# First FFN's up-projection by one level of Strassen's scheme, on one NeuronCore

## The chip, the cores and the metric

The kernel runs on one NeuronCore of a Trainium2 chip. The metric is device time in microseconds for one execution of the whole program, as the median of several runs. The engines are TensorE (matmul; PE in the profile, its weight loads PEld), VectorE (DVE), ScalarE (ACT), GpSimd (POOL) and SyncE (SP), which here issues all DMAs. TensorE writes to PSUM, which ScalarE and VectorE read; GpSimd works on SBUF alone.

## The reference

Two layers of a hybrid backbone: 256 context tokens and 512 latent tokens (768 together, `T`), width 1024. Layer 0 is differential attention beside RWKV-7 with a ConvFFN, layer 1 a bidirectional Mamba-2 mixer with a ConvFFN. The change concerns the ConvFFN of layer 0, which runs on all 768 tokens:

```python
FFN_HIDDEN = 2816

def conv_ffn(h, w_up, conv_w, conv_b, w_down):
    val, gate = jnp.split(h @ w_up, 2, axis=-1)
    gate = dwconv_centred(gate, conv_w, conv_b)      # 3 taps along the tokens
    return (jax.nn.silu(gate) * val) @ w_down

# layer 0, for latent and for context tokens
h_lat = modulate(rmsnorm(x_lat, norm_ffn[i]), sh2_l, sc2_l)
x_lat = x_lat + g2_l * conv_ffn(h_lat, ffn_w_up[i], ...)
```

The hidden width 2816 is 22 tiles of 128, so the up-projection has 22 gate tiles and 22 value tiles, each the product of a 1024 x 128 slice of `w_up` with the 1024 x 768 input, and the down-projection has 8 output tiles over 22 input tiles.

## The kernel before

All activations lie transposed: features on the 128 partitions, tokens along the free axis. A product in full precision is made of three matmuls in `fp32r`: weights and activations are each split into a high part (a ScalarE copy to `fp32r`) and a low part (the remainder, by VectorE or GpSimd, function `split`), and the kernel sums high x high, high x low and low x high in PSUM. So an up-projection tile is 8 blocks of 128 input features x 3 matmuls, each over 768 tokens. A matmul's output stays within one PSUM bank of 512 columns, and `DSEG = ((256, 0, NCTX), (512, NCTX, T))` cuts the 768 tokens into a piece of 256 (context) and one of 512 (latent). A dense PSUM tile is 1024 columns, two banks, and the FFN has three of them in turn (`dense_ps`).

`wload` (L192) loads a weight slice of 512 KB by SP into one of two buffers `ws`; `split` writes `wh` (L134, ScalarE) and `wl` (L150, VectorE), two buffers each. `mm3` (L208) does the matmuls of a tile.

`ffn` runs three groups of 8, 8 and 6 hidden tiles. For each hidden tile `j` it makes the gate tile, applies bias and three taps (one ScalarE instruction and four VectorE instructions, read from PSUM, into `fg`), the silu, then makes the value tile, multiplies (L137, VectorE) and splits the product into `ah` and `al`. After a group come its down-projection tiles: 8 tiles of output, each `nk` blocks x 3 matmuls, added to the residual stream by two VectorE instructions (`residual`, L146, one for each token segment with its own modulation). The first three tiles (gate 0, value 0, gate 1) run while the norm before is still being applied: `seg_start` works through a first segment of tokens (L1143, and L1169 for the third tile) while the second segment's `NormMod.steps` modulate it. The last group's down-projection (L1207) goes through `seg_tail`, which interleaves it with the sums of squares (L319), the broadcast of the norm's row (L277) and the modulation of the next norm; its first two output tiles run together (`pair`), over all blocks but the last first.

The program is written in one order; a planner in the tile framework then fixes each engine's own order and the buffers when the program is built, by which instruction is ready first, and among ready ones by the order of the program. On the chip each engine follows that fixed order.

The mixer of layer 1 has the same pieces of 256 and 512 (L1427); its `dt` projection (L1774) alone uses pieces of 384.

## Time and profile before

| | |
|---|---|
| runs | 2375.05, 2375.70, 2380.39 us; median 2375.7 |
| profiled execution, span | 2375.0 us (the lowest of the runs is 0.05 above it) |
| TensorE busy | 2219.4 us, 93% |
| VectorE, ScalarE, GpSimd busy | 58%, 42%, 14% |
| first FFN, by the chain | about 826 to 1390 us |
| its full up-projection and down-projection after the first tiles | 853.0 to 1336.4 us as one unbroken chain of matmuls |
| DMA, mean of the core | 91 GB/s |

The page's slices are fortieths of the span, about 59 us each, so the first FFN is slices 14 to 23. A matmul's busy time overlaps that of the next one, since matmuls are pipelined; the distance from start to start is what it costs in a full stream.

### The profile page before, as it was taken

The page shows a single profiled execution, that of the slowest core. Times are in us where ns is not written, and L with a number is a line of the kernel's source. Part 1 is how long each engine was busy: PE and PEld are TensorE (multiplying, and loading weights), DVE is VectorE, ACT ScalarE, POOL GpSimd, SP SyncE. Part 2 cuts the span into 40 slices and gives each one's busy share as a digit, 9 for nine tenths or more (in the row PEclk, how much of TensorE's full clock was granted, in tenths as well). Part 3 has the DMA queues.
Part 4 walks back from the last instruction along what each step waited for, and adds up shares of the span by engine and source line. Part 5 has one row for each costly group of instructions (what it writes and reads, how often), then busy time and mean ns, then how long its engine had stood idle before and what let it go on. Part 6 is the DMA issues. An engine that isn't in the chain of part 4 may idle for free.

```text
span 2375.0 us, 38460 instructions
## 1 busy us (share of the span) xinstructions
PE 2219.4 (93%) x15644; PEld 1876.9 (79%) x15644; DVE 1382.7 (58%) x2513; ACT 1003.5 (42%) x1904; POOL 341.1 (14%) x358
## 2 busy tenths in 40 slices
PE   6989998688879899999999998999999998999998
PEld 4878887576768788888888886878788877888887
DVE  4777737848585643333323468867676666434445
ACT  4655538474743442122212345544444544323233
POOL 2000006242500110000000022223222123000000
PEclk9999999799979999999999999999899999999999
DMA  8111222767455512222222301111111112333332
GB/s 276 47 43 49 90 98 78 227 205 231 126 174 152 157 55 62 62 62 64 61 64 61 97 23 45 45 45 54 54 54 54 36 45 63 107 96 95 95 97 88
DMA packets 302128, 216.09 MB, mean 91 GB/s; under 512 B 8832, under 2 KB 272640, under 8 KB 301952
## 3 DMA queue, kind: packets, MB, share of 16 engines
q1 hardware_dynamic: 301952, 213.64, 29.8%
q8 instruction: 123, 2.02, 0.4%
q14 instruction: 53, 0.43, 0.1%
HBM read 197.36 MB, written 16.25 MB: 90 GB/s over the span
## 4 chain that ended last, share of the span: by engine, by line
PE 77%; DVE 11%; ACT 5%; DMA 3%; issue 2%; POOL 1%; SPq 1%; DVEq 0%; ACTq 0%; POOLq 0%
PE dps L208 41%; PE dps L1427 9%; PE dps L1207 3%; PE dps L1420 3%; DMA aws<-in_ada_w 2%; PE adaps L957 1%; PE g L724 1%; PE aps L983 1%; PE dps L1143 1%; PE tps L517 1%; DVE cv L146 1%; PE g L673 1%; PE c L851 1%; DVE gl L137 1%; DVE xw L137 1%
## 5 line engine op out<-in xcount | busy, mean ns | idle before, releaser
L134 ACT ACTIVATE wh<-ws 128x1024 fp32r<-128x1024 f32 x196 | 207.9, 1061 | 605.8 <-PE dps L208 469.5
L208 PE MATMUL dps<-hl,wh 128*128 128x256 f32 (+1 forms) x1368 | 402.1, 355 | 0.0
L208 PE MATMUL dps<-hh,wh 128*128 128x256 f32 (+1 forms) x1368 | 399.9, 353 | 1.1 <-ACT vT L134 0.9
L208 PE MATMUL dps<-hh,wl 128*128 128x256 f32 (+1 forms) x1368 | 400.8, 355 | 0.0
L208 PEld LDWEIGHTS dps<-hh,wl 128*128 128x128 f32 x1368 | 257.2, 189 | 37.9 <-issue 0.3
L150 DVE TENSOR_TENSOR wl<-ws,wh 128x1024 fp32r<-128x1024 f32 x136 | 166.7, 1226 | 205.9 <-ACT wh L134 201.9
L208 PEld LDWEIGHTS dps<-hh,wh 128*128 128x128 f32 x1368 | 257.2, 190 | 37.0 <-ACT vT L134 1.3
L208 PEld LDWEIGHTS dps<-hl,wh 128*128 128x128 f32 x1368 | 257.5, 189 | 35.0 <-issue 0.3
L1355 POOL TENSOR_TENSOR wl<-ws,wh 128x1024 fp32r<-128x1024 f32 x52 | 125.2, 2409 | 320.5 <-ACT wh L134 273.2
L1427 PE MATMUL dps<-hh,wh 128*128 128x256 f32 (+1 forms) x448 | 146.9, 380 | 15.4 <-DVE sz L146 13.6
L1427 PE MATMUL dps<-hh,wl 128*128 128x256 f32 (+1 forms) x448 | 142.8, 371 | 0.0
L1427 PE MATMUL dps<-hl,wh 128*128 128x256 f32 (+1 forms) x448 | 142.6, 370 | 0.0
L146 DVE SCALAR_TENSOR_TENSOR cv<-dps,cwh,cv 128x511 f32<-128x511 f32 (+3 forms) x176 | 109.6, 623 | 30.6 <-ACT cv L134 28.1
L208 PE MATMUL dps<-al,wh 128*128 128x512 f32 (+1 forms) x384 | 116.4, 358 | 0.0
L208 PE MATMUL dps<-ah,wl 128*128 128x512 f32 (+1 forms) x384 | 116.1, 357 | 0.0
L208 PE MATMUL dps<-ah,wh 128*128 128x512 f32 (+1 forms) x384 | 114.9, 354 | 0.0
L137 DVE TENSOR_TENSOR fg<-fg,dps 128x768 f32<-128x768 f32 (+1 forms) x44 | 36.1, 821 | 133.0 <-PE dps L208 130.3
L1427 PEld LDWEIGHTS dps<-hh,wh 128*128 128x128 f32 x448 | 86.8, 197 | 32.0 <-DVE sz L146 15.0
L1427 PEld LDWEIGHTS dps<-hh,wl 128*128 128x128 f32 x448 | 87.8, 197 | 13.6
L1427 PEld LDWEIGHTS dps<-hl,wh 128*128 128x128 f32 x448 | 87.9, 197 | 12.9
L146 DVE SCALAR_TENSOR_TENSOR fg<-dps,par,fg 128x511 f32<-128x511 f32 (+1 forms) x132 | 85.1, 658 | 16.4 <-ACT fg L134 14.0
L146 DVE SCALAR_TENSOR_TENSOR x<-dps,mod,x 128x256 f32<-128x256 f32 (+1 forms) x56 | 31.9, 594 | 104.1 <-PE dps L208 102.3
(575 smaller groups left out, 4546.0 us busy)
## 6 DMA issues: line engine op xcount, KB each, us to landing
aws<-in_ada_w SPq DMA_DIRECT2D x96, 512.0 KB, 5.0
ws<-in_ffn_w_up SPq DMA_DIRECT2D x88, 512.0 KB, 3.8
ws<-in_ssm_w_in SPq DMA_DIRECT2D x40, 512.0 KB, 3.9
ws<-in_ffn_w_down SPq DMA_DIRECT2D x32, 512.0 KB, 3.6
ws<-in_ev_w_in SPq DMA_DIRECT2D x26, 512.0 KB, 4.0
ws<-in_ssm_w_out SPq DMA_DIRECT2D x16, 512.0 KB, 3.4
ws<-in_ffn_w_down SPq DMA_DIRECT2D x16, 384.0 KB, 3.1
projd<-tsh SPq DMA_DIRECT2D x12, 384.0 KB, 2.6
```

Of the source, the lines that this page charges most:

```text
L134: S.activation(out=o, in_=i, func=func, bias=bias, scale=scale, **kw)
L137: V.tensor_tensor(out=o, in0=x, in1=y, op=op)
L146: V.scalar_tensor_tensor(out=o, in0=x, scalar=s, in1=y, op0=op0, op1=op1)
L150: eng.tensor_tensor(out=lo, in0=src, in1=hi.bitcast(F32), op=ALU.subtract)
L208: PE.matmul(ps[:, po:po + hi - lo], lhsT=w[:, k0 + k, :], rhs=x[:, xk0 + k, lo:hi], start=(first and k == 0 and j == 0), stop=(last and k ...
L517: PE.matmul(po[:, 0:n], lhsT=w[:, kk, :], rhs=xx[:, kk, 0:n], start=(kk == 0 and j == 0), stop=(kk == nk // 128 - 1 and j == 2))
L673: PE.matmul(zp[:, mm], lhsT=lora[:, d, m * 128:(m + 1) * 128], rhs=wv, start=True, stop=True)
L724: PE.matmul(gp[:, m, :], lhsT=g1[:, m, cl].rearrange("p s t -> p (s t)"), rhs=z[:, m, par_, :], start=True, stop=True)
L1207: PE.matmul(ps[:, off + lo:off + hi], lhsT=w[:, k, :], rhs=x_[:, lo:hi], start=(k == 0 and j == 0), stop=(k == nk - 1 and j == 2))
L1355: G.tensor_tensor(out=lo, in0=w, in1=hi.bitcast(F32), op=SUB)
L1420: PE.matmul(ps[:, 512 * h:512 * h + 512], lhsT=w[:, k, h * 128:(h + 1) * 128], rhs=x[k], start=(k == 0 and j == 0), stop=(k == 3 and j == 2))
L1427: PE.matmul(ps[:, po:po + hi - lo], lhsT=w[:, k, :], rhs=x[:, k, lo:hi], start=(k == 0 and j == 0), stop=(k == KD - 1 and j == 2))
```

## The change

In layer 0's FFN, `ffn` is replaced by `ffn_fast`. Pairs 0 and 1 (value and gate tile of one hidden tile) stay plain. For the other 20 pairs the product of the 256 x 1024 weights (value and gate rows) with the 1024 x 768 input is taken as a 2 x 2 by 2 x 2 block product (blocks: value/gate; first and second half of the input features; first and second 384 tokens) in the Winograd form of Strassen's scheme: seven half products instead of eight, each 4 blocks x 3 matmuls over 384 columns.

- The input's sums and differences are made once (`NormHalf` and `operands`): GpSimd adds high and low parts of the first 384 tokens back together, VectorE makes four differences for each of four feature blocks, and they are split into high and low parts.
- The weights' sums are made for every pair (`fast`): two GpSimd and two VectorE instructions of 512 columns, and a third split, of 1536 columns. The split sums lie in columns 384 to 768 of the first four blocks of `hs`, which no product reads.
- The seven products are combined into value and gate in SBUF: two ScalarE copies, five VectorE sums that read PSUM, two GpSimd sums. The taps then read the gate from SBUF.
- Each product takes half a dense PSUM tile.
- The groups become (0,3), (3,6), (6,10), (10,14), (14,18), (18,22). The down-projection loads weights for two output tiles at a time (`wsplit2`) in the first five groups; the last one runs every output tile by segment, without `pair`.
- Pieces of 256 and 512 become two of 384 in layer 0's input projection, in the FFN and in the mixer (`DSEG`, `XS`), and PSUM offsets move from 256 to 128 for them. The norm ahead of the FFN has segments of 384 (context and the first 128 latent tokens; the other 384).
- The residual stream is held in two tiles, `xc` (context) and `xl` (latent), from the start, loaded by 16 DMAs instead of 8; the weight pool `wsp` is opened once for layer 0's tail and once for layer 1.

```diff
+SEG_MID = (((1, 0, NCTX), (0, NCTX, T // 2)), (0, T // 2, T))
...
-        DSEG = ((256, 0, NCTX), (512, NCTX, T))
+        DSEG = ((128, 0, T // 2), (512, T // 2, T))
...
+        class NormHalf(NormMod):
+            def steps(self, si):
...
+                for q in range(4):
+                    yield
+                    u = self.alloc(F32).rearrange("p (i t) -> p i t", i=2)
+                    for i in range(2):
+                        k = q + 4 * i
+                        stt(u[:, i], self.xv(k, lo, hi), am[:, self.layer, self.which, k, c:c + 1], rs, MUL, MUL)
+                        act(u[:, i], u[:, i], AF.Identity, bias=mod[:, self.layer, 24 * self.which + k, c:c + 1])
+                    split(hh[:, q:q + 5:4, lo:hi], hl[:, q:q + 5:4, lo:hi], u, G)
+                    self.h1.append(u)
+                for q in range(4):
+                    v = self.alloc(F32).rearrange("p (i t) -> p i t", i=2)
+                    G.tensor_tensor(out=v, in0=hh[:, q:q + 5:4, 0:lo].bitcast(F32), in1=hl[:, q:q + 5:4, 0:lo].bitcast(F32), op=ADD)
+                    self.h0.append(v)
+
+            def operands(self):
...
+                    tt(v[:, 0], u[:, 0], v[:, 0], SUB)
+                    tt(u[:, 0], u[:, 1], u[:, 0], SUB)
+                    tt(u[:, 1], u[:, 1], v[:, 0], SUB)
+                    tt(v[:, 1], v[:, 1], u[:, 1], SUB)
...
+                        split(hi, lo, f)
...
+            def prod(w, x):
+                ps = half_ps()
+                for q in range(4):
+                    xh, xl_ = x(q)
+                    for j, (w_, x_) in enumerate(((w[0], xh), (w[0], xl_), (w[1], xh))):
+                        PE.matmul(ps, lhsT=w_[:, q, :], rhs=x_, start=q == 0 and j == 0, stop=q == 3 and j == 2)
+                return ps
...
+            def fast(j):
+                w1 = wload(up[:, j * 128:(j + 1) * 128], KD, 128)
+                w2 = wload(up[:, (NH + j) * 128:(NH + j + 1) * 128], KD, 128)
+                s = pool.tile([128, 4, 3, 128], F32, tag="sw", name="sw", bufs=1)
+                G.tensor_tensor(out=s[:, :, 0], in0=w2[:, 0:4], in1=w2[:, 4:8], op=ADD)
+                tt(s[:, :, 1], s[:, :, 0], w1[:, 0:4], SUB)
+                G.tensor_tensor(out=w2[:, 0:4], in0=w1[:, 0:4], in1=w2[:, 0:4], op=SUB)
+                tt(s[:, :, 2], w1[:, 4:8], s[:, :, 1], SUB)
+                (h1, l1), (h2, l2) = ([wsp.tile([128, 8, 128], F32R, tag=tg, name=tg, bufs=2) for tg in ("wh", "wl")] for _ in range(2))
+                sh, sl = (x[:, 0:4, H:n].rearrange("p k (i m) -> p k i m", i=3) for x in hs)
+                split(h1, l1, w1)
+                split(sh, sl, s)
+                split(h2, l2, w2)
+                g, v, t = fg(), fg(), fg()
+                p5 = pnq.tile([128, 512], F32, tag="nt", name="p5", bufs=3)[:, 0:H]
+                v0, v1, g0, g1 = v[:, 0:H], v[:, H:n], g[:, 0:H], g[:, H:n]
+                act(v0, prod((h1[:, 0:4], l1[:, 0:4]), quad(0, 0)), AF.Copy)
+                act(p5, prod((sh[:, :, 0], sl[:, :, 0]), diff(0, 0)), AF.Copy)
+                tt(v1, v0, prod((sh[:, :, 1], sl[:, :, 1]), diff(1, 1)), ADD)
+                tt(v0, v0, prod((h1[:, 4:8], l1[:, 4:8]), quad(1, 0)), ADD)
+                tt(g1, v1, prod((h2[:, 0:4], l2[:, 0:4]), diff(1, 0)), ADD)
+                G.tensor_tensor(out=v1, in0=v1, in1=p5, op=ADD)
+                tt(v1, v1, prod((sh[:, :, 2], sl[:, :, 2]), quad(1, 1)), ADD)
+                tt(g0, g1, prod((h2[:, 4:8], l2[:, 4:8]), diff(0, 1)), ADD)
+                G.tensor_tensor(out=g1, in0=g1, in1=p5, op=ADD)
+                gate_tail(j, g, t)
+                tt(t, t, v, MUL)
+                return t
+
+            for j0, j1 in ((0, 3), (3, 6), (6, 10), (10, 14), (14, 18), (18, 22)):
...
-                    nm1, fw = ffn(0, x, nm0, fw, SEG_ALL, T, DSEG, pf, next0, prep1, lambda m, si: xsrc(m, *SEG_ALL[si][1:]))
+                    nm1, fw = ffn_fast(0, xv0, nm0, fw, SEG_ALL, T, pf, next0, prep1)
...
-                XS = ((256, 0, NCTX), (512, NCTX, T))
+                XS = ((128, 0, T // 2), (512, T // 2, T))
```

More of the change, by code (lines that the diff above doesn't have):

```diff
@@ L305, in __init__, with add @@
                 self.acc = pool.tile([128, n], F32, tag="nacc" + nm, name="nacc", bufs=1)
-            def add(self, xk):
-                if self.first:
-                    act(self.acc, xk, AF.Square)
-                else:
+            def add(self, *xs):
+                sq = self.acc
+                if not self.first:
                     sq = self.pool.tile([128, max(512, self.n)], F32, tag="nt", name="nsq", bufs=3)[:, 0:self.n]
-                    act(sq, xk, AF.Square)
+                o = 0
+                for xk in xs:
+                    act(sq[:, o:o + xk.shape[-1]], xk, AF.Square)
+                    o += xk.shape[-1]
+                if not self.first:
                     tt(self.acc, self.acc, sq, ADD)
@@ L1076, in add @@
             def add(self, m, si):
-                self.sq[si].add(self.xv(m, *self.segs[si][1:]))
+                self.sq[si].add(*[self.xv(m, lo, hi) for c, lo, hi in self.segs[si]])
             def rows(self, si):
@@ L1081, in rows @@
                     self.banks = (self.psf(), self.psf())
-                c, lo, hi = self.segs[si]
-                sums = self.banks[0 if self.segs[0][2] - self.segs[0][1] < self.segs[1][2] - self.segs[1][1] else 1]
-                return self.sq[si].finish(sums[:, 256 + 64 * si:320 + 64 * si], self.banks[si][:, 0:hi - lo])
+                ns = [hi - lo for lo, hi in self.span]
+                sums = self.banks[0 if ns[0] < ns[1] else 1]
+                return self.sq[si].finish(sums[:, 384 + 64 * si:448 + 64 * si], self.banks[si][:, 0:ns[si]])
@@ L1086, in steps @@
             def steps(self, si):
                 rs = self.rows(si)
-                c, lo, hi = self.segs[si]
+                s0 = self.span[si][0]
                 for k in range(KD):
                     yield
-                    modulate1(self.pool, self.xv(k, lo, hi), self.hs, rs, self.layer, self.which, c, k, lo, hi)
+                    for c, lo, hi in self.segs[si]:
+                        modulate1(self.pool, self.xv(k, lo, hi), self.hs, rs[:, lo - s0:hi - s0], self.layer, self.which, c, k, lo, hi)
@@ L1145, in dense_block, with wsplit2, ffn @@
             return f
+        def wsplit2(src, k, m):
+            w, hi, lo = (wsp.tile([128, 8, 128], t, tag=tg, name=tg, bufs=2).rearrange("p k m -> p (k m)")[:, 0:k * m].rearrange("p (k m) -> p k m", m=m)
+                         for tg, t in (("ws", F32), ("wh", F32R), ("wl", F32R)))
+            SY.dma_start(out=w, in_=src.rearrange("(k p) m -> p k m", p=128))
+            split(hi, lo, w)
+            return hi, lo
         def upw(layer, col, eng=V):
             return wsplit(a["ffn_w_up"][layer][:, col * 128:(col + 1) * 128], KD, eng)
[L1150 removed]
+        def ffn(layer, xv, nm, fw, segs, n, msegs, pool, make_next, prep_next):
             off = 1024 - n
[L1152 removed]
+            moff = msegs[0][0] - msegs[0][1]
+            hs = nm.hs
             dn = a["ffn_w_down"][layer]
```

224 lines of the change are left out of this document (169 added, 55 removed).

## The prediction

> **What bounds the kernel now.** I read the page first (busy shares, slices), then the busy time by stretch, then the chain of waits, then the groups by shape.
>
> ```profile
> PE 2219.4 (93%) x15644; PEld 1876.9 (79%) x15644; DVE 1382.7 (58%) x2513; ACT 1003.5 (42%) x1904; POOL 341.1 (14%) x358
> ...
> PE   6989998688879899999999998999999998999998
> ...
> PEclk9999999799979999999999999999899999999999
> ...
> 853.00:970.00 117.00, 117.00 (x664) 101.41 (x664) 45.89 (x57) 32.99 (x36) 0.00 (x0) 1.00 0.22 64
> ...
> 1346.00:1395.00 49.00, 47.95 (x272) 41.64 (x271) 29.69 (x54) 20.04 (x33) 3.62 (x4) 1.00 0.24 65
> ```
>
> The slices show TensorE full in the middle, where the first FFN lies. The stretch 853 to 970 us (up-projection of the first group; columns: length, busy PE, PEld, DVE, ACT, POOL, granted clock, DMA share, GB/s) has TensorE busy for 117.00 of 117.00 us at full clock, VectorE for 39%, GpSimd for none; in 1346 to 1395 (last down-projection and the start of the next norm) only 1.05 us are idle. So this stage costs its matmuls and nothing else. What one matmul costs is read from the chain, which runs through them back to back:
>
> ```profile
> 815.97 2.44 PE dps L208 x10
> ...
> 818.41 0.44 PE rsps L277 x4
> ...
> 853.00 483.36 PE dps L208 x2736
> ...
> 1412.09 7.30 PE rsps L1774 x42
> ...
> L1774 PE MATMUL rsps<-hh,wd 128*128 128x384 f32 x32 | 7.3, 336 | 0.0
> ```
>
> Third row: 483.36 us / 2736 = 176.7 ns, the mean of a 256 and a 512 column piece. Fourth: 7.30 / 42 = 173.8 ns for a 384 column piece (shape in the fifth row). 768 columns cost 353.3 ns now and 347.6 ns in two pieces of 384.
>
> **The change, TensorE's part.** Before: 44 up tiles of 48 matmuls and 22 x 8 x 3 x 2 = 1056 down matmuls, 3168 x 176.7 = 559.7 us. After: two plain pairs 4 x 48 = 192; twenty pairs of 7 products x 4 x 3 = 84, 1680; down-projection of the first five groups 18 x 48 = 864. These 2736 are 384 wide: 475.5 us. The last group keeps its segments of 512 and 256, 192 matmuls at the mean of both forms, 33.9 us. Together 509.4, so **-50.3 us of TensorE time**; 47.2 of it is the scheme (96 x 176.7 = 16.96 against 84 x 173.8 = 14.60 us a pair).
>
> The Trainium skill ("TensorE: Matmul & The Clock Gate", § Wait — 56ns, not 53.3ns?) puts a warm matmul at N/2.4 GHz plus about 2.5 ns. By it both cuts of 768 columns cost 325 ns, the pieces bring nothing, and the scheme brings 20 x 12 x 162.5 ns = 39 us (an estimate from that page; the total would be 11 us later, 2367). The rows here show 173.8 and 176.7 ns, so the trace disagrees and decides.
>
> **The vector engines' part.** This is what the scheme pays with.
>
> ```profile
> L150 DVE TENSOR_TENSOR wl<-ws,wh 128x1024 fp32r<-128x1024 f32 x136 | 166.7, 1226 | 205.9 <-ACT wh L134 201.9
> ...
> L150 DVE TENSOR_TENSOR wd<-wdt,wd 128x1536 fp32r<-128x1536 f32 x1 | 1.7, 1744 | 0.0
> ...
> L146 DVE SCALAR_TENSOR_TENSOR fg<-dps,par,fg 128x511 f32<-128x511 f32 x88 | 65.8, 747 | 15.6 <-ACT fg L134 14.0
> ...
> L146 DVE SCALAR_TENSOR_TENSOR fg<-dps,par,fg 128x255 f32<-128x255 f32 x44 | 21.1, 479 | 0.8
> ...
> L150 DVE TENSOR_TENSOR al<-fg,ah 128x768 fp32r<-128x768 f32 x22 | 20.9, 952 | 0.9 <-ACT ah L134 0.9
> ...
> L150 DVE TENSOR_TENSOR al<-fg,ah 128x512 fp32r<-128x512 f32 x22 | 15.1, 685 | 1.4 <-ACT ah L134 1.4
> ...
> L137 DVE TENSOR_TENSOR hst<-hst,sps 128x512 f32<-128x512 f32 x12 | 8.2, 681 | 1.4 <-PE sps L1598 0.8
> ...
> L137 DVE TENSOR_TENSOR st<-c,st 128x256 f32<-128x256 f32 x22 | 9.2, 418 | 21.1 <-PE c L851 21.1
> ...
> L134 ACT ACTIVATE wh<-ws 128x1024 fp32r<-128x1024 f32 x196 | 207.9, 1061 | 605.8 <-PE dps L208 469.5 <-issue 63.0 <-PE dps L1427 38.4
> ...
> L134 ACT ACTIVATE wd<-wdt 128x1536 fp32r<-128x1536 f32 x1 | 1.5, 1493 | 0.1
> ...
> L134 ACT ACTIVATE fg<-dps,par 128x768 f32<-128x768 f32 x22 | 21.5, 978 | 2.3 <-PE dps L208 2.3
> ...
> L134 ACT ACTIVATE ah<-fg 128x768 fp32r<-128x768 f32 x22 | 18.6, 848 | 12.3 <-DVE fg L137 12.2
> ...
> L1355 POOL TENSOR_TENSOR wl<-ws,wh 128x1024 fp32r<-128x1024 f32 x52 | 125.2, 2409 | 320.5 <-ACT wh L134 273.2 <-PE dps L1427 12.2 <-DVE er L141 10.4
> ...
> 393.96 1.29 POOL L699 TENSOR_TENSOR br<-kd,slr 128x512 f32<-128x512 f32 x1
> ...
> 394.00 1.80 DVE L137 TENSOR_TENSOR g<-ta,sg 128x512 f32<-128x512 f32 x1 [0.18 <-ACT sg L134]
> ...
> 505.52 3.25 POOL L819 TENSOR_TENSOR st<-st,wc 128x256 f32<-128x256 f32 x1 [4.19 <-DVE vv L137]
> ...
> 505.82 0.68 DVE L146 SCALAR_TENSOR_TENSOR ta<-ta,slkk 128x512 f32<-128x512 f32 x1
> ...
> 507.62 0.68 DVE L137 TENSOR_TENSOR g<-kd,sg 128x512 f32<-128x512 f32 x1
> ```
>
> VectorE per fast pair, both inputs in SBUF: two sums of 512 (2 x 0.685), low halves of w1 and w2 (2 x 1.226) and of the sums (1.744), taps, now from SBUF (2 x 0.69 + 2 x 0.42, by the 512 row and the 256 row; the PSUM rows 747 and 479 ns are the upper end), product and low half (2 x 0.952): 9.7 us. Five evacuations of 384 with one PSUM input, between 0.418 and 0.681, 0.55 each: 2.75. Sum **12.4 us of 14.6**, against 39% now. GpSimd: two of 512 (1.29) and two of 384 (by the 512 and 1024 rows 1.29 and 2.41, 2.2 ns a column: 1.02): **4.6 us**. ScalarE: 2 x 1.061 + 1.493 + 0.978 + 2 x 0.848 and two copies of about 0.49: 7.3 us, not a bound.
>
> The 394.00 row matters: a VectorE operation that takes 0.685 took 1.80, because GpSimd was at 393.96 in a two-input operation of 1.29; at 505.52 it is the other way round, GpSimd stretched to 3.25 while VectorE's operations, back to back, kept 0.68. Two-input work from SBUF on the two engines excludes itself: 9.7 + 4.6 = **14.3 us of exclusive time in a pair of 14.6**. It fits only because a group also has a down-projection (4 x 48 x 173.8 ns = 33.4 us), into which the last pair's tail and the first pair's preparation spread.
>
> **What TensorE then waits for.** Each wait has cover and price; engine changes cost 0.04 to 0.1 us, and the reader of a finished sum starts 0.27 us after TensorE goes on:
>
> ```profile
> 1081.44 0.52 PE L208 MATMUL dps<-hh,wl 128*128 128x256 f32 x2
> ...
> 1081.79 0.51 PE L208 MATMUL dps<-hh,wh 128*128 128x256 f32 x2
> ...
> 1082.06 0.95 DVE L137 TENSOR_TENSOR fg<-fg,dps 128x768 f32<-128x768 f32 x1 [4.23 <-PE dps L208]
> ...
> 1083.05 0.85 ACT L134 ACTIVATE ah<-fg 128x768 fp32r<-128x768 f32 x1 [0.35 <-DVE fg L137]
> ...
> 1388.79 0.37 SPq L1765 DMA_DIRECT2D wdt<-in_ssm_w_in  x1
> ...
> 1390.57 0.54 POOL L1764 MEMSET wdt<- 128x512 f32 x1
> ...
> ws<-in_ffn_w_up SPq DMA_DIRECT2D x88, 512.0 KB, 3.8
> ```
>
> *Pair to pair.* The split sums have one buffer, in unused columns of `hs`. It is free when product 6 ends; product 2 of the next pair needs it: 1.49 + 1.74 + 0.1 = 3.33 us, under products 7 and 1, 4.17 us. Slack 0.84. (Reads of other columns of `hs` don't hold it: the load into the middle columns of `wdt` at 1388.79 did not wait for the clearing of its neighbours at 1390.57.) The sums are ready in time: w2's buffer is free some 3 us into the pair, 0.4 + 3.8 to land, 1.29 + 2 x 0.685 to add: 10 of 12.5 us. In VectorE's queue either a low half (1.23) or GpSimd's lock (1.29) can stand in front; both together cost 1.29 + 1.23 - 0.84 = 1.7. Range 0 to 1.7 a pair (no gain possible: TensorE's work is counted). Ordering the four pairs of a group by when each input is ready gave a wait at about two pairs, 0.4 on average: **8.5 us**, nearer the lower end because the slack row counts for every pair and the collisions for some.
>
> *Turn into the down-projection*, five times and once at the end: the last activation comes after 0.27 + 0.55 + 1.02 + 0.98 + 2.2 + 0.85 + 0.95 + 0.85 + 0.95 + 0.4 = 9.0 us behind product 7; with one or two splits of the down weights in between, 10.7. Before it was 0.95 + 0.85 + 0.95 behind seven other blocks. Cover, as three PSUM tiles can hold sums without the last block: 3 x 18 matmuls, 9.4 us (groups of four), 6.3 (of three), about 5.2 (last, pieces of 512, 256, 512: 9 x 0.58). That TensorE's order may run ahead like this shows at 815.97: ten matmuls of the next tile stand before L277's, which the program issues earlier but which wait for a small chain. I take 3 x 1.7, 2 x 3 and 5.5: **16.6 us** (9.4 with the bare chain, 23 with a lock in each).
>
> *Head.* The operand differences cost VectorE 16 x 0.56 + 8 x 0.952 = 16.5 us, GpSimd 8 x 1.85 (768 columns, between the rows of 512 and 1024) and 2 x 1.3 for the third tile, all exclusive, under 144 x 173.8 ns = 25.0 us of first tiles, which hold all three PSUM tiles. The fourth, pair 1's value, starts when gate 0's taps have left the queue: I take **7 us** (0 if they go first, 15 if last).
>
> *End.* The last group has 4 blocks an item instead of 6, so TensorE covers 2.8 us less of the next norm, which VectorE paces: **2.8** (0 to 5).
>
> *Elsewhere.* 384 pieces: 26 + 18 tiles of layer 0 and the mixer x 24 x 5.7 ns = 6.0 us; TensorE is not full there, I take **-5** (-6 to 0). Residuals and squares cut at token 384: 8 x 0.4 us more on VectorE in a tail that waits for it, **+1** (0 to 3). Moved PSUM offsets, eight more loads of x (0.37 us each on SP, under the output projection) and the second weight pool (under the 25 us of the mixer's first tiles): nothing; uncovered, 3 us.
>
> **Sum.** -50.3 + 8.5 + 16.6 + 7 + 2.8 - 5 + 1 = -19.4 us. The profiled span is 2375.0, the median of the runs 0.7 above: 2375.0 - 19.4 + 0.7 = **2356 us**.
>
> **Rivals.**
> *TensorE stays covered*: no pair waits, head 0, bare chain at the turns (9.4): 23 us less of waits, 2333. For it: VectorE's average over a group is (4 x 12.4 + 4 x 1.23 for the down weights + 8 x 1.2 for residuals, by the tap rows)/91.8 = 70%. Against: the 0.84 us of slack.
> *The lock sets the pace*: each pair pays 1.7 (+25.5) and each turn's chain, which crosses from VectorE to GpSimd and back, 2 more (+12): 2393, slower. It decides from 1.4 us a pair on (0.4 + 20/20). For it the 394.00 row and 14.3 of 14.6; against it the 507.62 row: back-to-back VectorE work keeps its pace, and evacuations from PSUM don't need the lock. The Trainium skill ("SBUF — State Buffer", § SBUF: two separate sides) has the same rule, that whichever of the two starts first holds the shared ports for its whole instruction; both places in the trace agree with it.
> *Down-projection in strict order*: TensorE sits at the first tile's last block, cover 3.1, 2.1 and 2.0 us (18, 12 and 9 matmuls), waits 3 x 7.6 + 2 x 8.6 + 8.7 = 48.7 instead of 16.6: 2388, slower. Against it 815.97.
>
> **How the numbers follow.** Forecast (2340 to 2368) 0.52, covered 0.16, lock 0.17, strict order 0.09, otherwise near no change 0.06. Faster by over 0.3% (7 us, about what a measurement of this kernel can tell): 0.52 + 0.16 = 0.68. The lock's case spreads from 2375 to 2393, half of it within 0.3%: same 0.15, slower 0.17. Range 2332 to 2390: from the covered case to the strict order, short of the full lock.
>
> **What would show it.** Product matmuls 174 ns apart; VectorE near 80% and GpSimd near 30% in the up stretches; TensorE's gaps before product 2 (released by VectorE's low half of the sums), before each group's fourth block, and before pair 1's value. Wrong if gaps stand before most products (lock) or if each turn shows 7 us.

## The result, and the profile after

The changed kernel takes 2451.9 us (median of 4 runs, 2440.7 to 2454.0); the kernel before, on the same chip, 2377.3 us. The ratio is **1.030, 95% interval 1.028 to 1.033**: slower by 75 us, where 20 us faster was forecast. The profiled executions differ by 64 us (spans 2439.0 and 2375.0; the one after is the shortest of its four runs), and everything below that comes from traces is reckoned on these. The experiments ran on several chips, so each ratio is to the kernel before on the same chip, and a difference of a few microseconds between two medians can be one of chips.

The busy shares and the slices of the page after:

```profile
PE 2207.5 (91%) x15404; PEld 1946.1 (80%) x15404; DVE 1574.9 (65%) x2767; ACT 1062.5 (44%) x1996; POOL 459.3 (19%) x444
...
PE   6999997798878889998989788999999998999998
...
DVE  4767656667675776666666577966676776434445
...
PEclk9999999899979989999999899989999999999999
```

TensorE did 240 instructions fewer, and is idle for longer. In slices 14 to 24, the first FFN, the nines of before have become a mix of 8 and 9, with a 7 in the 23rd, where the last turn lies; the granted clock falls to 8 in the 15th (the head) and in the 23rd.

The busy time by stretch (length, busy PE, PEld, DVE, ACT, POOL, granted clock, DMA share, GB/s), first before: the head of the FFN, a stretch of pairs, the last down-projection with the norm.

```profile
826.00:853.00 27.00, 26.89 (x161) 23.86 (x161) 16.30 (x27) 15.75 (x24) 14.51 (x10) 1.00 0.12 35
1040.00:1130.00 90.00, 90.00 (x512) 78.06 (x511) 35.85 (x45) 25.52 (x28) 0.00 (x0) 1.00 0.22 65
1336.00:1404.00 68.00, 65.36 (x364) 56.07 (x364) 42.44 (x74) 27.41 (x45) 6.19 (x6) 1.00 0.21 58
```

The same three places after:

```profile
825.00:883.00 58.00, 41.15 (x205) 38.67 (x205) 48.95 (x74) 30.90 (x52) 25.02 (x18) 0.85 0.08 25
1040.00:1130.00 90.00, 84.36 (x470) 81.06 (x471) 58.50 (x74) 28.11 (x32) 17.22 (x13) 1.00 0.20 59
1389.00:1457.00 68.00, 53.86 (x264) 43.73 (x264) 45.90 (x80) 30.43 (x49) 13.57 (x9) 0.90 0.27 74
```

In the pairs VectorE is busy for 65%, not the forecast 80%, and GpSimd for 19%, not 30%; yet TensorE stands idle there. In the head and at the end the granted clock is 0.85 and 0.90 where it was 1.00; in this stretch of pairs it stays at 1.00.

What TensorE waited for in the first FFN after (line, releaser: us in total, times, longest):

```profile
PE dps L1349 <- DVE fg L138: 32.0, 28, 2.2
PE dps L1190 <- POOL hl L151: 12.8, 6, 4.2
PE dps L1421 <- ACT a L135: 8.4, 1, 8.4
PE dps L209 <- DVE fg L147: 6.4, 1, 6.4
PE dps L1433 <- ACT a L135: 5.7, 5, 1.7
...
PE dps L1349 <- DVE wl L151: 3.3, 3, 1.1
```

L1349 are the products; `fg L138` is the VectorE sum that takes a product out of PSUM. So the products mostly wait for a free half of a PSUM tile, 28 times, and seldom for split weights. L1190 is the head, waiting for the low halves that GpSimd makes of the norm's second segment (10.4 of the 12.8 us; the rest stands at the mixer's first tiles, which come from the same line); L209 is pair 1's value; L1433 and L1421 are the turns into the down-projection.

A table sums this up, for this kernel and the experiments. Every start-to-start distance of TensorE between the first FFN's first matmul and the start of the mixer's `dt` projection is cut in three: the pitch of its form (173.7 ns for 384 columns, 227 for 512, 119.7 for 256) with small differences is work; what lies over the pitch where the next matmul shows idle time is wait; what lies over it by more than 80 ns without idle time is slow. Slow distances are matmuls at half clock, and also, at full clock, the first matmul behind an idle stretch, some 0.1 us over its pitch, and other small losses. The last column is the rest of the program behind that point.

| profiled execution | first FFN, us | work | waits | slow | rest |
|---|---|---|---|---|---|
| before | 578.4 | 572.1 | 3.7 | 2.5 | 970.9 |
| after | 632.4 | 525.1 | 84.8 | 22.5 | 981.4 |
| old place of the weight pool | 644.7 | 529.8 | 84.4 | 30.5 | 967.3 |
| all four sums on VectorE | 597.7 | 524.8 | 52.9 | 20.0 | 982.6 |
| data sums on VectorE | 619.7 | 525.3 | 70.5 | 23.8 | 982.9 |
| weight sums on VectorE | 612.7 | 525.2 | 66.7 | 20.8 | 982.3 |
| four sums, old place, head's low halves | 592.3 | 529.4 | 45.3 | 17.6 | 968.4 |
| four sums, old place, two-part split | 593.3 | 528.8 | 46.0 | 18.4 | 969.8 |
| all of these, pair 21 plain | 578.5 | 531.1 | 35.2 | 12.3 | 970.7 |
| ... and pair 2 plain | 572.6 | 533.0 | 25.0 | 14.6 | 966.3 |
| ... and groups 4, 4, 4, 4, 6 | 559.4 | 529.5 | 21.4 | 8.5 | 969.7 |
| last experiment (reference's values) | 573.9 | 530.7 | 31.3 | 11.9 | 970.3 |
| 384-column pieces alone | 568.8 | 563.1 | 3.3 | 2.4 | 971.5 |

(In all rows with the scheme and the old place of the weight pool but the one with groups 4, 4, 4, 4, 6, that is in the third, the seventh to tenth and the one of the last experiment, 40 matmuls of 256 columns of the mixer's first tiles stand ahead of the `dt` projection instead of behind it: about 5 us moved from the last column to the first.) So the change did save 47.0 us of TensorE's work. It paid with 81.1 us of waits, 20.0 us of slow matmuls, and 10.5 us behind the FFN, in code that it hardly touched. Of the 22.5 us of slow distances after, about 12 lie where the granted clock was 0.50 (5 in the head, 3 in pairs and turns, 4 at the end); in the kernel before none does.

### The profile page after: what moved, and what is told of

The parts are those of the page before. It is cut to its first block, busy times and chain, and to the rows that moved or that the text cites. A ratio compares the mean times of both kernels' runs of the same rounds, so it can differ in the third digit from the quotient of the medians.

```text
span 2439.0 us, 38619 instructions
## 1 busy us (share of the span) xinstructions
PE 2207.5 (91%) x15404; PEld 1946.1 (80%) x15404; DVE 1574.9 (65%) x2767; ACT 1062.5 (44%) x1996; POOL 459.3 (19%) x444
## 4 chain that ended last, share of the span: by engine, by line
PE 62%; DVE 17%; ACT 6%; issue 6%; DMA 5%; POOL 3%; SPq 1%; POOLq 0%; ACTq 0%; DVEq 0%
PE dps L209 21%; PE dps L1637 8%; PE dps L1349 5%; PE dps L1433 3%; PE dps L1630 3%; DMA ws<-in_ffn_w_up 2%; DMA aws<-in_ada_w 2%; DVE wl L151 1%; DVE fg L138 1%; PE dps L1262 1%; PE adaps L961 1%; PE g L728 1%; ACT hh L135 1%; PE aps L987 1%; DVE cv L147 1%
## 5 line engine op out<-in xcount | busy, mean ns | idle before, releaser
L135 ACT ACTIVATE wh<-ws 128x1024 fp32r<-128x1024 f32 (+1 forms) x200 | 210.1, 1051 | 463.4 <-PE dps L209 198.8
L209 PE MATMUL dps<-hh,wh 128*128 128x384 f32 (+1 forms) x728 | 237.8, 369 | 7.7 <-DVE fg L147 6.4
L209 PE MATMUL dps<-hh,wl 128*128 128x384 f32 (+1 forms) x728 | 239.8, 370 | 1.3 <-DVE wl L151 1.3
L209 PE MATMUL dps<-hl,wh 128*128 128x384 f32 (+1 forms) x728 | 239.7, 369 | 0.0
L151 DVE TENSOR_TENSOR wl<-ws,wh 128x1024 fp32r<-128x1024 f32 (+1 forms) x142 | 177.7, 1251 | 94.7 <-ACT wh L135 82.7
L1637 PE MATMUL dps<-hh,wh 128*128 128x384 f32 (+1 forms) x448 | 148.0, 382 | 15.9 <-DVE sz L147 14.2
L138 DVE TENSOR_TENSOR fg<-fg,dps 128x384 f32<-128x384 f32 (+2 forms) x124 | 71.3, 580 | 138.5 <-PE dps L1349 81.6
L209 PEld LDWEIGHTS dps<-hh,wh 128*128 128x128 f32 x728 | 135.0, 191 | 24.6 <-issue 7.2
L209 PEld LDWEIGHTS dps<-hh,wl 128*128 128x128 f32 x728 | 135.2, 190 | 17.5 <-DVE wl L151 1.6
L209 PEld LDWEIGHTS dps<-hl,wh 128*128 128x128 f32 x728 | 135.5, 190 | 16.2 <-issue 0.3
L1637 PE MATMUL dps<-hl,wh 128*128 128x384 f32 (+1 forms) x448 | 144.7, 373 | 0.0
L1637 PE MATMUL dps<-hh,wl 128*128 128x384 f32 (+1 forms) x448 | 142.1, 369 | 0.0
L1433 PE MATMUL dps<-a,wh 128*128 128x384 f32 x576 | 124.5, 336 | 5.7 <-ACT a L135 5.7
L1433 PEld LDWEIGHTS dps<-a,wh 128*128 128x128 f32 x576 | 101.6, 188 | 7.8 <-ACT a L135 7.3
L1637 PEld LDWEIGHTS dps<-hh,wh 128*128 128x128 f32 x448 | 85.4, 197 | 27.6 <-DVE sz L147 15.7
L1349 PE MATMUL dps<-a,wh 128*128 128x384 f32 x320 | 85.9, 347 | 17.1 <-DVE fg L138 17.0
L1637 PEld LDWEIGHTS dps<-hh,wl 128*128 128x128 f32 x448 | 86.2, 197 | 7.9
L1637 PEld LDWEIGHTS dps<-hl,wh 128*128 128x128 f32 x448 | 86.8, 198 | 6.7
L1349 PE MATMUL dps<-a,hh 128*128 128x384 f32 x320 | 85.2, 342 | 1.9 <-ACT fg L135 1.2
```

The costliest lines, as they stand in the source:

```text
L135: S.activation(out=o, in_=i, func=func, bias=bias, scale=scale, **kw)
L138: V.tensor_tensor(out=o, in0=x, in1=y, op=op)
L151: eng.tensor_tensor(out=lo, in0=src, in1=hi.bitcast(F32), op=ALU.subtract)
L209: PE.matmul(ps[:, po:po + hi - lo], lhsT=w[:, k0 + k, :], rhs=x[:, xk0 + k, lo:hi], start=(first and k == 0 and j == 0), stop=(last and k ...
L1349: PE.matmul(ps, lhsT=w_[:, q, :], rhs=x_, start=q == 0 and j == 0, stop=q == 3 and j == 2)
L1433: PE.matmul(ps[:, p_:p_ + hi - lo], lhsT=w_[:, k, :], rhs=x_[:, lo:hi], start=(k == 0 and j == 0), stop=(k == nk - 1 and j == 2))
```

## The experiments

**1. The rest of the program: where the weight pool lies.** Layer 1's FFN is not changed, yet was longer. One stretch of 100 us of unbroken 512-column matmuls in it, before, after, and in the first experiment:

```profile
2025.00:2125.00 100.00, 100.00 (x443) 82.81 (x442) 44.32 (x50) 30.68 (x37) 0.00 (x0) 1.00 0.32 95
```

```profile
2085.00:2185.00 100.00, 100.00 (x428) 80.43 (x427) 42.33 (x49) 29.81 (x35) 0.00 (x0) 1.00 0.32 95
```

```profile
2085.00:2185.00 100.00, 100.00 (x443) 82.81 (x442) 45.10 (x51) 31.67 (x38) 0.00 (x0) 1.00 0.32 95
```

443 against 428 matmuls at full clock with TensorE never idle: 226 ns each against 234.

```diff
+        wsp = es.enter_context(tc.tile_pool(name="wspm", bufs=2))     # beside phs, once
         pnq = es.enter_context(tc.tile_pool(name="pnq", bufs=1))
...
-            wsp = e3.enter_context(tc.tile_pool(name="wspf", bufs=2))
...
-            wsp = es.enter_context(tc.tile_pool(name="wspm", bufs=2, side="right"))
```

> The changed kernel with one thing undone: the weight pool lies where the kernel before has it (beside the norm's input tiles, open once), instead of in one pool for layer 0 and one at the far end of the memory for layer 1. The scheme stays. Theory 'place': layer 1's FFN was unchanged and yet 9.8 us longer (411.8 to 421.6), its 512-column matmuls 234 ns apart instead of 227; with the old place they return to 227, the part from the first FFN's end on gets 10 to 13 us shorter, total near 2440. Rival 'aftermath' (the slower pitch comes from something that the first FFN leaves behind, or from the new pieces): 234 ns stays, 2452.

2440.9 us (ratio to before 1.026, 1.024 to 1.029), 11 less than the changed kernel; the third stretch above has 443 matmuls again. The place of the pool is the cause, shown by the pitch, here and in experiments 2 and 3. Why matmuls are slower with the pool at that place isn't known; no run moved it anywhere else, and the pool holds the loaded weights as well as their split halves. The mixer's 384-column pieces showed the same 173 to 174 ns with either place.

**2 and 3. The pieces alone, with either place.** The scheme is left out: `ffn` in place of `ffn_fast`, the norm's old segments; the rest of the change stays.

```diff
-                    nm1, fw = ffn_fast(0, xv0, nm0, fw, SEG_ALL, T, pf, next0, prep1)
+                    nm1, fw = ffn(0, xv0, nm0, fw, SEG_ALL, T, DSEG, pf, next0, prep1)
```

> Pieces alone: no scheme, the old groups of 8, 8 and 6, the old place of the weight pool; two pieces of 384 columns in layer 0's input projection, the first FFN and the mixer. By the prediction's rows (176.7 ns against 173.8) the FFN gives 7.3 us (2528 full-stream matmuls x 2.9), layer 0's projection 3 and the mixer 2.5: near 2364. Rival 'pieces bring nothing' (the pitch of 384 depends on the weight pool's place too): 2377.

> Pieces alone as in the run beside it, but with the weight pools where the changed kernel has them. Theory 'place': layer 1's 512-column matmuls are 234 ns apart, 12 us longer than the run beside it, near 2376. Rival 'aftermath of the scheme': same as the run beside it, 227 ns.

2375.3 us (0.998, 0.997 to 1.000) and 2380.0 (1.002, 1.000 to 1.004). The far place costs in both kernels: in the profiled executions 8.2 us from the `dt` projection to the end (972.2 and 980.4), in the medians 4.8, less than the 12 expected. The first run missed its forecast: its FFN was 8.6 us shorter (569.8), but the output projection ahead of it, with the residual stream in two tiles, was 4.7 us longer (46.3 from 41.6). Experiment 9 takes up that part.

**4 to 6. The lock.** What the waits for PSUM look like in the changed kernel's timeline (start, length, engine, operation; idle before it and its releaser in brackets):

```profile
1134.24 0.69 DVE L138 TENSOR_TENSOR sw<-sw,ws 128x512 f32<-128x512 f32 x1 [1.25 <-POOL sw L1383]
1134.29 1.78 POOL L1385 TENSOR_TENSOR ws<-ws 128x512 f32<-128x512 f32 x1
...
1134.85 0.55 DVE L138 TENSOR_TENSOR fg<-fg,dps 128x384 f32<-128x384 f32 x1
...
1135.32 1.57 DVE L151 TENSOR_TENSOR a<-fg,a 128x768 fp32r<-128x768 f32 x1
1136.81 0.54 DVE L138 TENSOR_TENSOR fg<-fg,dps 128x384 f32<-128x384 f32 x1
...
1137.41 0.62 PE L1349 MATMUL dps<-a,wh 128*128 128x384 f32 x2 [1.97 <-DVE fg L138]
```

GpSimd's sum of 1.29 us starts behind VectorE's and takes 1.78, as if it did not move until VectorE's ends at 1134.93. VectorE's sum out of PSUM at 1134.85 is not held up. The low half at 1135.32 is: 1.57 instead of 0.95, until GpSimd ends at 1136.07 and 0.8 more. The next evacuation stands behind it in VectorE's order, and TensorE, which needs that half of PSUM, has been idle for 1.97 us when it comes. The lock's part of that is 0.62 us. The first row shows a second way in which GpSimd holds up VectorE: VectorE's own weight sum needs GpSimd's first one, and VectorE stood idle for 1.25 us until it was there, with both evacuations behind it in its order. If GpSimd's sums are the cause, by the one way or the other, the same sums on VectorE, where they add to the work of the fuller engine, make the kernel faster:

```diff
-                G.tensor_tensor(out=s[:, :, 0], in0=w2[:, 0:4], in1=w2[:, 4:8], op=ADD)
+                tt(s[:, :, 0], w2[:, 0:4], w2[:, 4:8], ADD)
...
-                G.tensor_tensor(out=w2[:, 0:4], in0=w1[:, 0:4], in1=w2[:, 0:4], op=SUB)
+                tt(w2[:, 0:4], w1[:, 0:4], w2[:, 0:4], SUB)
...
-                G.tensor_tensor(out=v1, in0=v1, in1=p5, op=ADD)
+                tt(v1, v1, p5, ADD)
...
-                G.tensor_tensor(out=g1, in0=g1, in1=p5, op=ADD)
+                tt(g1, g1, p5, ADD)
```

> The changed kernel with the four GpSimd sums of a fast pair on VectorE instead. No lock between the two engines is left in a pair; VectorE has 2.5 us more, 14.9 us for each pair of 14.6 us of TensorE. Theory 'lock' (operations stretched by the exclusion hold up the sums that free PSUM): VectorE's operations take their short times again (0.95 instead of 1.57 for a low half of 768), waits fall by a third or more, 2410 to 2430. Rival 'VectorE's load and order': the engine is simply too full and its queue too long, waits grow, 2455 to 2480.

2412.5 us (1.015, 1.013 to 1.017): **39 us less, with 2.5 us more work for VectorE in every pair**, and 34.7 less in the first FFN's trace. Groups by shape in the pairs of the changed kernel, then with the sums on VectorE (instructions, busy us, mean ns, idle time before them):

```profile
L138 DVE TENSOR_TENSOR fg<-fg,dps 128x384 f32<-128x384 f32 x100 | 54.2, 550 | 93.7 <-PE dps L1349 81.6 <-POOL fg L1400 9.8 <-ACT fg L135 2.0
L151 DVE TENSOR_TENSOR hl<-sw,hh 128x1536 fp32r<-128x1536 f32 x19 | 39.8, 2096 | 3.9 <-ACT hh L135 3.4
...
L138 DVE TENSOR_TENSOR sw<-ws,sw 128x512 f32<-128x512 f32 x19 | 24.8, 1305 | 0.4
L151 DVE TENSOR_TENSOR a<-fg,a 128x768 fp32r<-128x768 f32 x20 | 22.1, 1107 | 6.8 <-ACT a L135 6.8
...
L138 DVE TENSOR_TENSOR sw<-sw,ws 128x512 f32<-128x512 f32 x19 | 13.2, 692 | 31.6 <-POOL sw L1383 31.6
...
L1385 POOL TENSOR_TENSOR ws<-ws 128x512 f32<-128x512 f32 x19 | 34.0, 1792 | 1.5
```

```profile
L151 DVE TENSOR_TENSOR hl<-sw,hh 128x1536 fp32r<-128x1536 f32 x20 | 35.0, 1752 | 2.8 <-ACT hh L135 2.5
...
L151 DVE TENSOR_TENSOR a<-fg,a 128x768 fp32r<-128x768 f32 x21 | 20.0, 954 | 6.7 <-ACT a L135 6.7
...
L138 DVE TENSOR_TENSOR sw<-ws 128x512 f32<-128x512 f32 x19 | 13.1, 690 | 22.5 <-DMA ws<-in_ffn_w_up 22.5
...
L138 DVE TENSOR_TENSOR sw<-ws,sw 128x512 f32<-128x512 f32 x19 | 13.0, 684 | 0.0
```

The last weight sum took 1305 ns on average beside GpSimd and takes 684 alone. Over all its rows in the pairs, VectorE's operations were about 27 us longer beside GpSimd than they would have been with this run's durations; that is the lock. VectorE also stood idle for GpSimd's results for 41.4 us (31.6 and 9.8 in the rows), where it now stands 22.5 for the weights' loads: some 19 us that came with the crossing from GpSimd to VectorE. Two runs with one half of the edit each:

> The changed kernel with only the two data sums (v1 + p5 and g1 + p5, 384 columns) on VectorE; the two weight sums stay on GpSimd. GpSimd's work in a pair falls from 4.6 to 2.6 us by the prediction's rows. Theory 'lock' (each GpSimd sum stretches what runs beside it on VectorE, wherever it stands): a bit under half of the 39 us that came with all four sums, near 2434. Rival 'hop' (what costs is the crossing VectorE, GpSimd, VectorE inside the chain that frees PSUM, 2.1 us for a sum that takes 0.5 on VectorE): nearly all of it, near 2415.

> The changed kernel with only the two weight sums (512 columns) on VectorE; the two data sums stay on GpSimd. Theory 'lock': a bit over half of the 39 us, near 2430. Rival 'hop': little, 2445 or more.

2434.6 us (1.027, 1.024 to 1.029) and 2427.1 (1.024, 1.020 to 1.027): 17 and 25 us less than the changed kernel in the medians, but only about 9 and 15 by the ratios (37 for both at once); these runs were on another chip than experiment 4, and each interval reaches some 7 us to either side. The traces are the clearer evidence: the first FFN is 12.7 and 19.7 us shorter, 32.4 together against 34.7 for both at once. So the weight sums cost more than the data sums, and the crossing of the data sums alone is not it. The two runs do not tell the lock from every crossing, though: each half takes away its share of both, since VectorE waits in its order for GpSimd's weight sum too. Followed back along VectorE, from the sum that ended each of the 28 waits to the last point at which VectorE itself waited for TensorE, 11 waits have both behind them, 8 a wait for GpSimd's result alone and 3 the lock alone (counting 0.2 us and more). Shown is that GpSimd's sums make the products wait; how much of it is the lock stays open.

**7 and 8. The head, and the single buffer of the split sums.** Both with all four sums on VectorE and the weight pool at the old place.

```diff
-                    split(hh[:, q:q + 5:4, lo:hi], hl[:, q:q + 5:4, lo:hi], u, G)
+                    split(hh[:, q:q + 5:4, lo:hi], hl[:, q:q + 5:4, lo:hi], u)
```

> All four sums on VectorE, the weight pool at the old place (2412 - 11 = 2401 if the two add up), and in the head the low halves of the norm's second segment on VectorE instead of GpSimd (4 x 768 columns). Theory 'lock in the head too': TensorE's waits there for GpSimd's low halves (12.2 us with the sums on VectorE) shrink to a third, near 2393. Rival 'VectorE is full there' (50.7 us busy of 58): the wait moves to VectorE and to pair 1's value, 2399 to 2405.

```diff
-                split(sh, sl, s)
+                split(sh[:, :, 0:2], sl[:, :, 0:2], s[:, :, 0:2])
+                split(sh[:, :, 2], sl[:, :, 2], s[:, :, 2])
```

> All four sums on VectorE, the weight pool at the old place, and the split of the weight sums in two parts (1024 columns for products 2 and 3, 512 for product 6), so that the first part may be overwritten after product 3 instead of product 6. Theory 'single buffer' (the 0.84 us of slack of the prediction): the waits for the low half of the sums (3.5 us with the sums on VectorE) go, near 2396. Rival: those waits are a matter of VectorE's queue, and stay; 2401.

2388.4 us (1.007, 1.004 to 1.010) and 2396.5 (1.011, 1.007 to 1.014), against 2401 if neither did anything. That 2401 is a sum of two experiments' gains (2412 - 11), not a run. By it the head's GpSimd work cost more than expected, 13 us; the 4.5 us for the single buffer are within the interval and rest on the waits below. The head, in the changed kernel's timeline:

```profile
844.54 4.22 DVE L138 TENSOR_TENSOR a<-a,a 128x384 f32<-128x384 f32 x2 [2.50 <-POOL a L1120]
846.24 2.11 POOL L151 TENSOR_TENSOR hl<-a,hh 128x768 fp32r<-128x768 f32 x1
...
848.40 0.45 PE L1190 MATMUL dps<-hl,wh 128*128 128x384 f32 x1 [3.80 <-POOL hl L151]
```

Two VectorE operations of 384 columns, with two SBUF inputs, took 4.22 us together, while GpSimd worked without a pause on low halves and on sums for the operands; TensorE waited 3.80 us for one low half. GpSimd's operations of 768 columns took 1.80 to 1.84 us here before VectorE joined and 2.11 to 2.15 after, so the lock added about 0.3 to each; the rest of that wait is GpSimd's own queue, in which two sums stood ahead of the low half. The waits with the two-part split (all four sums on VectorE):

```profile
PE dps L1190 <- POOL hl L151: 11.4, 7, 3.8
PE dps L1422 <- ACT a L135: 7.9, 1, 7.9
PE dps L209 <- DVE fg L147: 6.2, 1, 6.2
...
PE dps L1349 <- DVE fg L138: 3.3, 5, 1.0
```

The products' wait for PSUM, 32.0 us in the changed kernel, is 3.3; the wait for low halves of the split sums (`hl` at L1349, 3.5 us without the two-part split) is gone. What is left are the last turn and the head, the two places where the scheme itself adds a chain.

**9. The pieces, without anything else.** The kernel before with the new cut, `DSEG` and `XS` of 384 columns and the PSUM offsets; nothing else.

```diff
-        DSEG = ((256, 0, NCTX), (512, NCTX, T))
+        DSEG = ((128, 0, T // 2), (512, T // 2, T))
...
-                XS = ((256, 0, NCTX), (512, NCTX, T))
+                XS = ((128, 0, T // 2), (512, T // 2, T))
```

> The kernel before with nothing changed but the pieces: 384 columns instead of 256 and 512 in layer 0's input projection, the first FFN and the mixer, with the PSUM offsets that this needs. The residual stream in one tile, its loads and the norm's segments stay (in the earlier run of pieces alone they were those of the changed kernel, and its output projection was 4.7 us longer than before). Theory: the first FFN gains its 8.6 us (as in that run's trace) and the projection 2, near 2366. Rival (the 4.7 us came from the pieces): 2375.

**2363.9 us (0.9955, 0.994 to 0.997)**, faster than both kernels. The same stretch of the first FFN, before (length, busy PE, granted clock, DMA share, GB/s) and in this kernel:

```profile
870.00:970.00 100.00, 100.00 (x568) 1.00 0.22 64
```

```profile
870.00:970.00 100.00, 100.00 (x579) 100.00 (x578) 38.81 (x48) 28.21 (x30) 0.00 (x0) 1.00 0.22 65
```

579 matmuls for 568 in 100 us, with the same mean number of columns: 172.7 ns each for 176.1. The FFN takes 568.8 us for 578.4. So in the FFN the cut into 384s is worth what the prediction's rows said. The output projection takes 44.3 us here, between the 41.6 of before and the 46.3 of the second experiment. One execution of each doesn't divide these 4.7 us between the cut and the two tiles: the third experiment, with the same code there as the second, took 45.2, and the changed kernel 39.1.

**10 to 12. Plain pairs where the chains are long.** These three have all four sums on VectorE, the old place of the weight pool, the head's low halves on VectorE and the two-part split. Their plain pairs behind the first fast pair (21; in the last also 20) read the columns of `hs` that hold the split sums by then, so their values are not the reference's; the instructions are those of a plain pair.

```diff
-                    t = (plain if j in first else fast)(j)
+                    t = (plain if j in (0, 1, 21) else fast)(j)             # 10
+                    t = (plain if j in (0, 1, 2, 21) else fast)(j)          # 11; operands() after pair 1
+                    t = (plain if j in (0, 1, 2, 20, 21) else fast)(j)      # 12
...
-            for j0, j1 in ((0, 3), (3, 6), (6, 10), (10, 14), (14, 18), (18, 22)):
+            for j0, j1 in ((0, 4), (4, 8), (8, 12), (12, 16), (16, 22)):    # 12
```

> Scheme with all four sums on VectorE, weight pool at the old place, head's low halves on VectorE, split of sums in two parts (2401 - 13 - 4.5, about 2384 if the parts add up), and pair 21 plain, so that the last turn into the down-projection no longer stands behind a fast pair's tail. Costs TensorE 2.4 us, takes most of 8.1 us of wait away: near 2379. Rival (the wait is that of any last activation): 2385.

> As the run beside it, and pair 2 plain too, with the operands' differences issued after pair 1 in the program. VectorE then has 17 us more of TensorE's time for the operands; pair 1's value need not wait 8.7 us for gate 0's taps. 2.4 us of TensorE for 6 to 8 of waits: near 2374. Rival (VectorE does the differences first all the same): 2381.

> As the run beside it, with groups of 4, 4, 4, 4 and 6 (one turn less, and a last down-projection of six blocks as before, which covers more of the next norm) and pairs 20 and 21 plain: 17 fast pairs. TensorE +2.4 us, turns and end -7: near 2370. Rival: 2376, no gain over the run beside it.

2378.4 us (1.001, 0.999 to 1.002), 2370.1 (0.998, 0.996 to 0.999) and 2359.8 (0.994, 0.991 to 0.996). The first came as expected, the other two 4 and 10 us better: with 17 fast pairs, short chains at head and turn, and no sums on GpSimd, waits and slow matmuls together are 29.9 us. That is faster than the kernel before, but the pieces alone (experiment 9) have 2363.9 and an interval that overlaps: a gain of the scheme itself is not shown. Waits in the second of them:

```profile
PE dps L1427 <- ACT a L135: 2.5, 1, 2.5
PE dps L209 <- DVE fg L147: 2.4, 1, 2.4
...
PE dps L1349 <- DVE fg L138: 0.8, 2, 0.5
```

The last turn (L1427) fell from 7.9 to 2.5, pair 1's value (L209) from 6.2 to 2.4. With a place of their own for the split sums, 12 KB a partition, such a kernel should have the right values; that wasn't run.

**13 to 16. The same with the reference's values.** Pairs 0, 1, 2 plain, 19 fast, all else as in 11. First the products in another order, the gate's first (in 13 to 15 the two weight tiles of a pair also take their buffers in the other order in every second pair):

```diff
+                tt(v1, v0, prod((sh[:, :, 1], sl[:, :, 1]), diff(1, 1)), ADD)
+                tt(g1, v1, prod((h2[:, 0:4], l2[:, 0:4]), diff(1, 0)), ADD)
+                tt(v1, v1, p5, ADD)
+                tt(g0, g1, prod((h2[:, 4:8], l2[:, 4:8]), diff(0, 1)), ADD)
+                tt(g1, g1, p5, ADD)
+                gate_tail(j, g, t)
+                tt(v0, v0, prod((h1[:, 4:8], l1[:, 4:8]), quad(1, 0)), ADD)
+                tt(v1, v1, prod((sh[:, :, 2], sl[:, :, 2]), quad(1, 1)), ADD)
```

> Pairs 0, 1, 2 plain and 19 fast, groups of the changed kernel, four sums on VectorE, old place of the weight pool, head's low halves on VectorE, split in two parts; and the products in another order: the gate's five first (1, 2, 3, 5, 7), then 4 and 6, so that taps and silu of the last pair run under two products and only its product and low half stand in the turn. Theory 'tail' (the wait before the last down-projection, 8 us with all these otherwise, is the chain behind product 7): the turns cost 4 to 5 us less in all, near 2368 (2370 of the run with pair 21 plain, +5.6 for its turn, -2.4 for one plain pair less, -4 to -5 here). Rival (the new order brings waits for the weights' buffers): 2375.

> As the run beside it, and the last down-projection begins with three output tiles over all 768 tokens, all blocks but the last first: cover of the last turn 9.4 us instead of 5.2. Theory 'cover': the rest of the last turn's wait goes, 3 to 4 us less than the run beside it, near 2365. Rival (the planner's order had it all the same, or the norm behind it becomes later): same as the run beside it.

> As the run with three output tiles, with groups 0-2, 2-6, 6-10, 10-14, 14-18, 18-22: the group of three with one fast pair goes. Expected within 2 us of the run beside it; a short first group has less cover in its turn (2 blocks: 6 matmuls x 3 tiles = 3.1 us).

2378.5 us (1.001, 0.999 to 1.002), 2380.1 (1.001, 0.999 to 1.003) and 2385.9 (1.003, 1.002 to 1.005): all three missed in the total, though three whole tiles made the FFN 3.3 us shorter in the trace (579.9 from 583.2). Waits of the first:

```profile
PE dps L1349 <- DVE fg L138: 10.1, 7, 2.4
PE dps L1427 <- ACT a L135: 3.6, 1, 3.6
```

The last turn is short, as expected, but the products now wait 10.1 us for PSUM, where 0.8 stood with the old order (last line of the fence above): the taps now stand in VectorE's order ahead of the sums of products 4 and 6, which may be the reason. So the new order for pair 21 alone, the buffers in the old order, and three whole tiles at the start of the last down-projection:

> 19 fast pairs, pairs 0, 1, 2 plain, every value computed as the reference asks. The old order of the products everywhere but in pair 21, which has the gate's five first; the last down-projection begins with three whole tiles; sums on VectorE, split in two parts, head's low halves on VectorE, weight pool at the old place. If the longer waits of the run with the new order in every pair came from the taps standing in VectorE's queue ahead of products 4 and 6 (10.1 us there, 0.8 with the old order), they go, and the short last turn (3.6 instead of 8) stays: near 2367, faster than the kernel before by 0.4%. Rival (the turns' gain was in the order of all pairs): 2374.

2377.6 us (1.001, 0.999 to 1.003). The products' wait fell to 3.3 us again and the last turn stayed at 4.7, as the reason given would have it, though the order of the buffers went back too. The FFN is 573.9 us with the 5 us that moved into it, so about 569, the same as with the pieces alone; the total is the same as before within the interval and, by the two ratios, some 13 us above the pieces alone. The profiled execution reached its first FFN only at 837.1 us, before at 825.7. That is no effect of this edit: kernels with the same code up to there (10 to 16) reached it between 824.4 and 837.1. So without sums on GpSimd and with the reference's values the scheme gives back what it costs, and no more, in the form tried.

## Why the prediction was wrong

**TensorE's work: right.** Forecast 50.3 us less in the FFN, measured 47.0 (572.1 to 525.1) up to the `dt` projection. Products 174 ns apart in a full stream, as said. The profile came out 83 us above the forecast of 19 us less; 36 of these are the pairs, 20 slow matmuls, 14 the rest of the program outside the FFN, 11 the waits of the head.

**"Pair to pair ... 0.4 on average: 8.5 us": this step failed.** By the start-to-start distances, the products waited about 44 us, over 2 us a pair, and 10 us of slow matmuls in pairs and turns came on top, under 3 of them at half clock. The step looked at one wait, the split sums' single buffer with 0.84 us of slack, and put GpSimd's lock into it as one collision of 1.29 us. That wait was real and small: 3.5 us in the trace with the sums on VectorE, gone in experiment 8, and 0.3 us in the changed kernel. What it left out is that every evacuation stands in VectorE's fixed order behind operations that the lock stretches and behind sums that wait for GpSimd's results, and that PSUM has no half to spare. The sum of exclusive time, 14.3 of 14.6 us, was taken as something that fits; with all sums on VectorE its rows add up to 14.9 us a pair and the kernel is 39 us faster.

**The rival "the lock sets the pace" happened in part**, beyond its price: 2393 was given, at 1.7 us a pair and 2 a turn. Experiments 4 to 6 show that GpSimd's sums set the pace; that the lock does it alone is not shown, since VectorE also stands idle for their results. The row that spoke against it, back-to-back VectorE work that keeps its pace, did not carry over: GpSimd got in while VectorE read PSUM at 1134.85, with no pause before VectorE's next operation, which then took 1.57 us instead of 0.95. The Trainium skill ("SBUF — State Buffer", § SBUF: two separate sides) says that whichever starts first keeps the shared ports for its whole instruction and the other fully blocks. The rows at 1134.24 to 1136.81 and at 844.54 agree.

**Turns, 16.6 us: right in the sum, partly by luck.** 5.7 and 8.4, 14.1 in all; the turn at the end, forecast 5.5, was 8.4, and the other five, forecast 11.1, were 5.7, so two errors cancelled. By the prediction's own chain of 10.7 us and its covers the five would have been 1.3 and 4.4 each, not the 1.7 and 3 that it took.

**Head, 7 us: too small.** Waits of 17.9 us and 5.8 of slow matmuls. Pair 1's value waited 6.4, as the step said; the 10.4 us for GpSimd's low halves of the norm's own second segment were in no term. Experiment 7, which takes these low halves off GpSimd, brought about 13 us by the sum above. The trace shows GpSimd busy without a pause from 840.9 to 856.7 with eight operations, five of them stretched by 0.3 us: mostly its own load, and only in the smaller part the lock.

**End, 2.8 us: too small** at some 8 (8 of waits beside the turn and 6.4 of slow matmuls, against 6.2 of both in the whole FFN before).

**"Moved PSUM offsets ... and the second weight pool: nothing": wrong by 11 us** in the medians, from the place of the weights (experiment 1). The 5 us that the pieces were to bring elsewhere do not show: in experiment 9 layer 0's input projection ran from 31.2 to 401.7 us (before 32.6 to 401.4), and what lies behind the FFN took 971.5 us (before 970.9).

**Slow matmuls: priced at nothing, 20.0 us more than before, about 12 of them at half clock.** No term had it. Half clock stands behind each of the four idle times of 3.8 us and more in the head and at the last turn, and behind two of the products' twelve waits of 1.8 to 2.2 us. Pair 1's value, after:

```profile
872.79 0.98 PE L209 MATMUL dps<-hh,wh 128*128 128x384 f32 x2 [6.41 <-DVE fg L147]
```

```profile
872.50:876.50 4.00, 3.71 (x12) 3.74 (x13) 4.00 (x8) 3.21 (x4) 1.18 (x1) 0.50 0.00 0
877.50:881.50 4.00, 4.00 (x25) 4.00 (x25) 1.33 (x2) 1.49 (x1) 0.00 (x0) 1.00 0.30 98
```

After 6.41 us of idle time the granted clock is 0.50 for four microseconds (12 matmuls), then 1.00 (25). A wait of 6.4 us thus cost about 8.5. The Trainium skill ("TensorE: Matmul & The Clock Gate", § Part 1: The HAM clock gate) says that an idle window of some 3.4 us halves the clock and a busy one of the same length restores it; the trace agrees here. At the 2 us measured here, half clock would have added some 4 us to the prediction's two long waits, the head's 7 and the last turn's 5.5 (an estimate).

Taken together, in the profiled executions: work -47.0, waits +81.1, slow matmuls +20.0, the rest behind the FFN +10.5, ahead of it -0.5: +64 us.

## What to carry to other kernels

A count of busy time on two engines that exclude each other is no proof that their work fits, even under the length of the stage: where the accumulators' release stands in one engine's fixed order, each collision there, and each result of the other engine that it has to wait for, can become a wait of TensorE. Before giving GpSimd a share of two-input SBUF work, price the same work on VectorE; here the fuller engine was the better place, by 39 us. And price every idle time of about 4 us and more with the half clock that follows it, and test a cut into equal pieces by itself: that part alone was worth 0.45%, and no form of the scheme with the reference's values did as well.
